# Attention logits of two head groups from half-height matmuls, value and retention products side by side

## The chip, the core and the metric

The kernel runs on one core of a Trainium2 chip. The metric is the device time of one execution in microseconds (us). TensorE multiplies (PE in the rows, with PEld for its weight loads), VectorE (DVE) and ScalarE (ACT) do the elementwise work, SyncE (SP) issues the DMAs. TensorE's results land in PSUM banks, which a program takes from a pool and gives back when the last reader is done.

## The reference, cut to what matters

Two layers over 256 tokens of width 1024. In each, one projection feeds eight attention heads (two groups g of four heads c; a group shares its keys and values) and eight retention heads:

```python
s_w = jnp.einsum('bqgrd,bgkd->bgrqk', qb, kwb)        # window branch; the selected branch likewise
p_w = masked_softmax(s_w - slopes[:, :, None, None] * dist_w, valid_w)
o_w = jnp.einsum('bgrqk,bgkd->bgrqd', p_w, vwb)
o = gb[0] * o_c + gb[1] * o_s + gb[2] * o_w           # gated sum of three branches
...
inner = jnp.einsum('bhnd,bhmd->bhnm', qi, ki) * decay_in   # retention
o = jnp.einsum('bhnm,bhme->bhne', inner, vi) + ...
```

With 256 tokens the selected branch picks every block and the window covers every key, so both are plain causal attention with a distance penalty. A dense SwiGLU follows in layer 0, eight experts (top 2) in layer 1, a gated per-layer embedding in both.

## The kernel before, in words

Everything runs in float32. Projections and other weight products are done as three fp32r products of a high and a low half (`mm3`, L207 to L209); the halves are made by ACT and DVE in `split` (L193, L194) from raw tiles that SP loads. Attention and retention use plain float32 products.

`mixer` does, in this order in the text: projections of values, keys and queries (`qT`, four tiles of 128 x 256, the two groups in partition halves); keys of the branches `br` 2 and 1 into `kz`, padded with zeros, so that group g's keys stand in its half of the partitions and the other half is zero; the compressed branch (L533 and after); then attention by query tile `t` (128 rows; t = 0 sees 128 keys, t = 1 sees 256), branch and group:

- logits, L572, four heads c as two pairs c2, each pair in one bank of `acc()`;
- row minima and the shifted logits, L576 on DVE, the exponential with its sum, L578 on ACT;
- scaling by gate over sum, L580 to L584 on DVE;
- transposes, L588, copied out of PSUM by ACT or DVE (L591, L593);
- the product with the values, L594, into half g of the columns of one bank;
- at the end of a tile the compressed branch's product, L604, and the copy into `mn` halves (L607, L608).

After attention come, in the text, three more projections that attention doesn't need: retention queries, keys and gates (240 products in all: 192 with 256 columns, 48 with 512). They take banks of `bank()`. Then retention: logits L648 and L657 over 64 partitions each, masked by decay on DVE (L650, L660), products with the values L668 and L670, and the output projection.

The order on each engine is set by a scheduler of the language, which moves instructions ahead of others in the text where their operands and buffers allow it. An engine executes its own queue in order. `bank()` and `acc()` are pools of four PSUM banks each, whose buffers are handed out in the order of the text: the fifth call gets the buffer of the first, once that is given back.

Of the kernel before, what the change touches and what calls it, by code (L numbers as in the profile page):

```python
# [92 lines left out]
def trunk(ctx: ExitStack, tc: tile.TileContext, a, cst, at, out, stop=None):  # L93
    nc = tc.nc
# [16 lines left out]
    def acc():  # L111
        w = psa.tile([128, 512], F32, name="acc")
        return w
# [267 lines left out]
    def mixer(i, pool, N, after, between, then, first, heads):  # L381
# [64 lines left out]
        kz = {}  # L446
        for br, src in ((2, pk[0]), (1, pk[1])):
            kz[br] = pool.tile([128, 2, S], F32, name=f"kz{br}")
            nc.gpsimd.memset(kz[br], 0.0)
            for g in range(2):  # L450
                gp = slice(g * 64, (g + 1) * 64)
                nc.vector.tensor_tensor(kz[br][gp, g], src[gp], R[gp], op=ALU.mult)
# [105 lines left out]
        for t in range(NT):  # L558
            nk = 128 * (t + 1)
            po = acc()  # L560
            pov = po.rearrange("p (c q) -> p c q", c=4)
            for bi, br in enumerate((2, 1)):
                for g in range(2):
                    P = brief.tile([128, 4, nk], F32, name="P", bufs=3)
                    mn = small.tile([128, 4], F32, name="mn")
                    sm = small.tile([128, 4], F32, name="sm")
                    for c2 in range(2):
                        pl = acc()
                        plv = pl[:, 0:2 * nk].rearrange("p (j k) -> p j k", j=2)
                        for j in range(2):  # L570
                            c = 2 * c2 + j
                            qk = nc.tensor.matmul(plv[:, j], qT[:, c, t * 128:(t + 1) * 128], kz[br][:, g, 0:nk],  # L572
                                             start=True, stop=True)
                        for j in range(2):
                            c = 2 * c2 + j
                            nc.vector.tensor_tensor_reduce(P[:, c], plv[:, j], K["dist"][:, 256 - nk:256], slope(g, c),  # L576
                                                           3e38, ALU.add, ALU.min, mn[:, c:c + 1])
                            nc.scalar.activation(P[:, c], P[:, c], AF.Exp, bias=mn[:, c:c + 1], scale=-1.0,  # L578
                                                 accum_out=sm[:, c:c + 1])
                    nc.vector.tensor_scalar(sm, sm, 1e-30, None, op0=ALU.max)  # L580
                    nc.vector.reciprocal(sm, sm)
                    nc.vector.tensor_tensor(sm, sm, gv[:, t, br, :, g], op=ALU.mult)
                    for c in range(4):
                        nc.vector.tensor_scalar(P[:, c], P[:, c], sm[:, c:c + 1], None, op0=ALU.mult)  # L584
                    for kc in range(t + 1):
                        pp = acc()
                        for c in range(4):
                            nc.tensor.transpose(pp[:, c * 128:(c + 1) * 128], P[:, c, kc * 128:(kc + 1) * 128], ident)  # L588
                        pT = brief.tile([128, 512], F32, name="pT", bufs=2)
                        if (g + kc) % 2:  # L590
                            nc.vector.tensor_copy(pT, pp)  # L591
                        else:
                            nc.scalar.copy(pT, pp)  # L593
                        nc.tensor.matmul(po[g * 64:(g + 1) * 64, :], vsw[:, kc, br - 1, g * 64:(g + 1) * 64], pT,  # L594
# [48 lines left out]
        A1 = pool.tile([128, 2, 4, 128], F32, name="xs")  # L643
        for s in range(2):
            p = acc()
            pw = p.rearrange("p (c n) -> p c n", c=4)
            for c in range(4):
# [709 lines left out]
```

## Time and profile before

| what | us |
|---|---|
| median of 3 runs | 1515.51 (1510.32 to 1520.99) |
| profiled execution, time | 1517.39 |
| its span, first to last instruction | 1515.6 |
| PE busy | 1449.3 (96%) |
| DVE busy, ACT busy | 642.1, 569.8 |
| mean granted TensorE clock | 0.987 |

Layer 0's mixer takes about 160 us of the span, layer 1's lies between 420 and 590 us, the experts fill the rest up to 1500 us, with the DMA engines near 100% busy there. A float32 matmul stands as two records in the trace, a transpose and an fp32r matmul as one. Records of PE overlap, so the distance from one start to the next tells what an instruction costs, not its length.

### The profile page before, as it was taken

To read this page: it belongs to the slowest core of one execution; us is meant where nothing else is said; L and a number is where in the kernel's file an instruction comes from. 1 tells how busy PE (TensorE), PEld (TensorE's weight loads), DVE (VectorE), ACT (ScalarE), POOL (GpSimd) and SP (SyncE) were. 2 spreads that over 40 slices of the span, in tenths; PEclk is the share of its full clock that TensorE was granted. 3 is DMA by queue.
4 is the path that set the end of the run, shared out by engine and by line. 5 is a ranking of instruction groups with operands and counts; after the bars stand their busy time and mean duration, and the time that the engine had idled before them with its cause. 6 is when DMAs were issued, how large, how long until landed. Compare 5 with 4: busy or idle time off the path is not lost. (4 is left out here: it accounts for less than half of the span.)

```text
span 1515.6 us, 30676 instructions
## 1 busy us (share of the span) xinstructions
PE 1449.3 (96%) x12570; PEld 832.9 (55%) x12570; DVE 642.1 (42%) x1459; ACT 569.8 (38%) x992; POOL 2.3 (0%) x8
## 2 busy tenths in 40 slices
PE   7999999999999999899999999999999999999987
PEld 6977899999889868433322232243333323323336
DVE  6765865555596767323222222222221322322337
ACT  5452544434464543333332332333233223223324
POOL 0000000000000000000000000000000000000000
PEclk9998999999999999899999999999999999999999
DMA  9923445555557513789999999999999999999971
GB/s 332 365 86 97 160 167 194 190 179 188 169 179 252 199 57 146 250 346 420 420 420 420 419 421 420 420 419 416 405 383 420 420 419 420 419 421 420 412 273 42
DMA packets 100621, 462.39 MB, mean 305 GB/s; under 512 B 9384, under 2 KB 20336, under 8 KB 57200
## 3 DMA queue, kind: packets, MB, share of 16 engines
q1 hardware_dynamic: 100224, 460.16, 77.5%
q8 instruction: 102, 1.67, 0.4%
q14 instruction: 55, 0.45, 0.1%
q10 hardware_dynamic: 240, 0.10, 0.0%
HBM read 459.19 MB, written 1.05 MB: 304 GB/s over the span
## 5 line engine op out<-in xcount | busy, mean ns | idle before, releaser
L1029 DVE COPY lo<-raw 128x512 f32 x333 | 140.7, 426 | 544.5 <-DMA raw<-in_moe_up 152.3
L1028 ACT COPY hi<-raw 128x512 f32 x333 | 204.0, 621 | 429.5 <-DMA raw<-in_moe_down 129.2
L194 DVE TENSOR_TENSOR lo<-raw,hi 128x1024 fp32r<-128x1024 f32 (+1 forms) x176 | 206.6, 1200 | 111.7 <-ACT hi L193 111.1
L193 ACT CAST hi<-raw 128x1024 fp32r<-128x1024 f32 (+1 forms) x176 | 175.0, 1031 | 170.0 <-issue 71.8
L1039 PE MATMUL w<-raw,xg 128*32 128x512 f32 x1744 | 211.5, 596 | 12.3 <-DMA raw<-in_moe_up 5.0
L1039 PE MATMUL acc<-raw,xg 128*32 128x512 f32 x1792 | 214.7, 596 | 2.5 <-DMA raw<-in_moe_gate 0.6
L207 PE MATMUL w<-xhi,hi 128*128 128x256 f32 x704 | 201.2, 286 | 0.3 <-ACT xhi L283 0.3
L209 PE MATMUL w<-xhi,lo 128*128 128x256 f32 x704 | 199.9, 284 | 0.0
L208 PE MATMUL w<-xlo,hi 128*128 128x256 f32 x704 | 199.7, 284 | 0.2 <-DVE xlo L284 0.2
L207 PEld LDWEIGHTS w<-xhi,hi 128*128 128x128 f32 x704 | 135.0, 192 | 2.4 <-issue 1.6
L208 PEld LDWEIGHTS w<-xlo,hi 128*128 128x128 f32 x704 | 135.0, 192 | 1.3 <-issue 0.8
L209 PEld LDWEIGHTS w<-xhi,lo 128*128 128x128 f32 x704 | 135.0, 192 | 0.8 <-issue 0.8
L1039 PE MATMUL acc<-raw,hT 128*32 128x512 f32 x960 | 116.6, 603 | 11.6 <-PEq L1225 6.6
L1039 PEld LDWEIGHTS w<-raw,xg 128*32 128x32 f32 x1744 | 51.8, 109 | 117.1 <-issue 66.2
L1039 PEld LDWEIGHTS acc<-raw,xg 128*32 128x32 f32 x1792 | 50.8, 109 | 98.7 <-issue 74.8
L1039 PE MATMUL w<-raw,hT 128*32 128x512 f32 x832 | 99.7, 597 | 4.8 <-DMA raw<-in_moe_down 1.4
L1039 PE MATMUL w<-hi,xg 128*32 128x256 f32 x448 | 72.8, 379 | 0.0
L1039 PE MATMUL w<-lo,xg 128*32 128x256 f32 x448 | 68.1, 379 | 0.0
L1039 PE MATMUL acc<-hi,xg 128*32 128x256 f32 x448 | 68.1, 379 | 0.0
L1039 PE MATMUL acc<-lo,xg 128*32 128x256 f32 x448 | 68.1, 379 | 0.0
L1039 PEld LDWEIGHTS acc<-raw,hT 128*32 128x32 f32 x960 | 28.4, 110 | 67.9 <-issue 38.0
L1039 PEld LDWEIGHTS acc<-hi,xg 128*32 128x32 f32 x448 | 27.6, 110 | 67.1 <-issue 55.9
(346 smaller groups left out, 1908.2 us busy)
## 6 DMA issues: line engine op xcount, KB each, us to landing
raw<-in_moe_gate SPq DMA_DIRECT2D x112, 1024.0 KB, 17.7
raw<-in_moe_down SPq DMA_DIRECT2D x112, 1024.0 KB, 17.8
raw<-in_moe_up SPq DMA_DIRECT2D x109, 1024.0 KB, 17.0
raw<-in_w_in SPq DMA_DIRECT2D x23, 1024.0 KB, 6.8
raw<-in_ffn_gate SPq DMA_DIRECT2D x14, 1024.0 KB, 5.1
raw<-in_ffn_up SPq DMA_DIRECT2D x14, 1024.0 KB, 5.1
raw<-in_ffn_down SPq DMA_DIRECT2D x14, 1024.0 KB, 5.0
raw<-in_cmp_w SPq DMA_DIRECT2D x8, 1024.0 KB, 8.8
```

What stands on the lines that cost most here:

```text
L193: order(nc.scalar.copy(hi[:, c], raw), b[0])
L194: order(nc.vector.tensor_tensor(lo[:, c], raw, hi[:, c].bitcast(F32), op=ALU.subtract), b[1])
L207: order(nc.tensor.matmul(o, l[0], r[0], start=start, stop=False, skip_group_check=skip), behind)
L208: nc.tensor.matmul(o, l[0], r[1], start=False, stop=False, skip_group_check=skip)
L209: nc.tensor.matmul(o, l[1], r[0], start=False, stop=stop, skip_group_check=skip)
L1028: nc.scalar.copy(hi, w[:, bass.ds(units[g][0], 1), :].rearrange("p e n -> p (e n)"))
L1029: nc.vector.tensor_copy(lo, w[:, bass.ds(units[g][1], 1), :].rearrange("p e n -> p (e n)"))
L1039: nc.tensor.matmul(P[b][o:o + UNIT, 0:WIDE[b]], x[:, b, o:o + UNIT], v, start=start, stop=stop, tile_position=(0, o), skip_group_check=True)
```

## The change

Keys are stored unpadded (`kT`, 128 x 256, both groups in their halves), so a group's logits are a product over 64 partitions instead of 128. The loop over groups moves inward: both groups' logits of a pair are issued alternately, group 0 into a bank of `acc()`, group 1 into one of `bank()`. The value products of the groups are issued next to each other, and so are retention's logits of the two partition halves. `P` and `pT` get four buffers, `mn` and `sm` too.

```diff
@@ -443,13 +443,10 @@
                     sp = R[g * 64:(g + 1) * 64, 0:1]
                     rv = bass.AP(tensor=sp.tensor, offset=sp.offset + par, ap=[sp.ap[0], [2, 16], [16, 15]])
                     nc.vector.tensor_tensor(dst, ap, rv, op=ALU.mult)
-        kz = {}
+        kT = {}
         for br, src in ((2, pk[0]), (1, pk[1])):
-            kz[br] = pool.tile([128, 2, S], F32, name=f"kz{br}")
-            nc.gpsimd.memset(kz[br], 0.0)
-            for g in range(2):
-                gp = slice(g * 64, (g + 1) * 64)
-                nc.vector.tensor_tensor(kz[br][gp, g], src[gp], R[gp], op=ALU.mult)
+            kT[br] = pool.tile([128, S], F32, name=f"kz{br}")
+            nc.vector.tensor_tensor(kT[br], src, R, op=ALU.mult)
 
 
         w = cols(1024, 512)
@@ -559,39 +556,45 @@
             nk = 128 * (t + 1)
             po = acc()
             pov = po.rearrange("p (c q) -> p c q", c=4)
+            rows = [slice(g * 64, (g + 1) * 64) for g in range(2)]
             for bi, br in enumerate((2, 1)):
-                for g in range(2):
-                    P = brief.tile([128, 4, nk], F32, name="P", bufs=3)
-                    mn = small.tile([128, 4], F32, name="mn")
-                    sm = small.tile([128, 4], F32, name="sm")
-                    for c2 in range(2):
-                        pl = acc()
-                        plv = pl[:, 0:2 * nk].rearrange("p (j k) -> p j k", j=2)
+
+                P = [brief.tile([128, 4, nk], F32, name="P", bufs=4) for g in range(2)]
+                mn = [small.tile([128, 4], F32, name="mn", bufs=4) for g in range(2)]
+                sm = [small.tile([128, 4], F32, name="sm", bufs=4) for g in range(2)]
+                for c2 in range(2):
+                    plv = [p[:, 0:2 * nk].rearrange("p (j k) -> p j k", j=2) for p in (acc(), bank())]
+                    for j in range(2):
+                        c = 2 * c2 + j
+                        for g in range(2):
+                            qk = nc.tensor.matmul(plv[g][:, j], qT[rows[g], c, t * 128:(t + 1) * 128],
+                                                  kT[br][rows[g], 0:nk], start=True, stop=True)
+                    for g in range(2):
                         for j in range(2):
                             c = 2 * c2 + j
-                            qk = nc.tensor.matmul(plv[:, j], qT[:, c, t * 128:(t + 1) * 128], kz[br][:, g, 0:nk],
-                                             start=True, stop=True)
-                        for j in range(2):
-                            c = 2 * c2 + j
-                            nc.vector.tensor_tensor_reduce(P[:, c], plv[:, j], K["dist"][:, 256 - nk:256], slope(g, c),
-                                                           3e38, ALU.add, ALU.min, mn[:, c:c + 1])
-                            nc.scalar.activation(P[:, c], P[:, c], AF.Exp, bias=mn[:, c:c + 1], scale=-1.0,
-                                                 accum_out=sm[:, c:c + 1])
-                    nc.vector.tensor_scalar(sm, sm, 1e-30, None, op0=ALU.max)
-                    nc.vector.reciprocal(sm, sm)
-                    nc.vector.tensor_tensor(sm, sm, gv[:, t, br, :, g], op=ALU.mult)
+                            nc.vector.tensor_tensor_reduce(P[g][:, c], plv[g][:, j], K["dist"][:, 256 - nk:256],
+                                                           slope(g, c), 3e38, ALU.add, ALU.min, mn[g][:, c:c + 1])
+                            nc.scalar.activation(P[g][:, c], P[g][:, c], AF.Exp, bias=mn[g][:, c:c + 1], scale=-1.0,
+                                                 accum_out=sm[g][:, c:c + 1])
+                for g in range(2):
+                    nc.vector.tensor_scalar(sm[g], sm[g], 1e-30, None, op0=ALU.max)
+                    nc.vector.reciprocal(sm[g], sm[g])
+                    nc.vector.tensor_tensor(sm[g], sm[g], gv[:, t, br, :, g], op=ALU.mult)
                     for c in range(4):
-                        nc.vector.tensor_scalar(P[:, c], P[:, c], sm[:, c:c + 1], None, op0=ALU.mult)
-                    for kc in range(t + 1):
+                        nc.vector.tensor_scalar(P[g][:, c], P[g][:, c], sm[g][:, c:c + 1], None, op0=ALU.mult)
+                for kc in range(t + 1):
+                    pT = []
+                    for g in range(2):
                         pp = acc()
                         for c in range(4):
-                            nc.tensor.transpose(pp[:, c * 128:(c + 1) * 128], P[:, c, kc * 128:(kc + 1) * 128], ident)
-                        pT = brief.tile([128, 512], F32, name="pT", bufs=2)
+                            nc.tensor.transpose(pp[:, c * 128:(c + 1) * 128], P[g][:, c, kc * 128:(kc + 1) * 128], ident)
+                        pT.append(brief.tile([128, 512], F32, name="pT", bufs=4))
                         if (g + kc) % 2:
-                            nc.vector.tensor_copy(pT, pp)
+                            nc.vector.tensor_copy(pT[g], pp)
                         else:
-                            nc.scalar.copy(pT, pp)
-                        nc.tensor.matmul(po[g * 64:(g + 1) * 64, :], vsw[:, kc, br - 1, g * 64:(g + 1) * 64], pT,
+                            nc.scalar.copy(pT[g], pp)
+                    for g in range(2):
+                        nc.tensor.matmul(po[rows[g], :], vsw[:, kc, br - 1, rows[g]], pT[g],
                                          start=(bi == 0 and kc == 0), stop=False, tile_position=(0, 64 * g),
                                          skip_group_check=True)
             if t == 0:
@@ -641,23 +644,22 @@
         nc.sync.dma_start(dec, cst["decay"])
         dv = dec.rearrange("p (s c n) -> p s c n", s=2, c=4)
         A1 = pool.tile([128, 2, 4, 128], F32, name="xs")
+        half = [slice(s * 64, (s + 1) * 64) for s in range(2)]
+        pw = [acc().rearrange("p (c n) -> p c n", c=4) for s in range(2)]
+        for c in range(4):
+            for s in range(2):
+                nc.tensor.matmul(pw[s][:, c], krT[half[s], c, 128:256], qrT[half[s], c, 128:256], start=True, stop=True)
         for s in range(2):
-            p = acc()
-            pw = p.rearrange("p (c n) -> p c n", c=4)
-            for c in range(4):
-                nc.tensor.matmul(pw[:, c], krT[s * 64:(s + 1) * 64, c, 128:256], qrT[s * 64:(s + 1) * 64, c, 128:256],
-                                 start=True, stop=True)
-            nc.vector.scalar_tensor_tensor(A1[:, s], pw, rs[1], dv[:, s, :, 0:128], op0=ALU.mult, op1=ALU.mult)
+            nc.vector.scalar_tensor_tensor(A1[:, s], pw[s], rs[1], dv[:, s, :, 0:128], op0=ALU.mult, op1=ALU.mult)
         for c2 in range(2):
+            pw = [acc().rearrange("p (c n) -> p c n", c=2) for s in range(2)]
+            for j in range(2):
+                c = 2 * c2 + j
+                for s in range(2):
+                    nc.tensor.matmul(pw[s][:, j], krT[half[s], c, 0:128], qrT[half[s], c, :], start=True, stop=True)
             for s in range(2):
-                p = acc()
-                pw = p.rearrange("p (c n) -> p c n", c=2)
-                for j in range(2):
-                    c = 2 * c2 + j
-                    nc.tensor.matmul(pw[:, j], krT[s * 64:(s + 1) * 64, c, 0:128], qrT[s * 64:(s + 1) * 64, c, :],
-                                     start=True, stop=True)
                 dc = dv[:, s, 2 * c2:2 * c2 + 2]
-                nc.vector.scalar_tensor_tensor(dc, pw, rs[0], dc, op0=ALU.mult, op1=ALU.mult)
+                nc.vector.scalar_tensor_tensor(dc, pw[s], rs[0], dc, op0=ALU.mult, op1=ALU.mult)
         cens = pool.tile([128, NT, 8, 64], F32, name="qrT")
         cen, var = [], pool.tile([128, NT, 8], F32, name="var")
         for t in range(NT):
```

The scheduler places much else anew. First place: PE's queue in layer 0 from the compressed branch's logits to the first value product of t = 0. `w_` are banks of `bank()`, `acc_` of `acc()`; L207 to L209 on `w_1022` and `w_1023` are the first of the 240 later projection products. Before:

```order
L533 MATMUL acc_670<-var_659,qT_517 128x32 x8
L572 MATMUL acc_700<-kz2_395,qT_517 128x128 x2
...
L572 MATMUL acc_707<-kz2_395,qT_517 128x128 x2
L207 MATMUL w_1022<-xhi_104,hi_1008 128x256
L208 MATMUL w_1022<-xlo_105,hi_1008 128x256
L209 MATMUL w_1022<-xhi_104,lo_1009 128x256
...
L588 MATMUL acc_721<-pack_80,P_697 128x128
...
L594 MATMUL acc_696<-pT_726,vsw_646 64x512
L572 MATMUL acc_732<-kz2_395,qT_517 128x128 x2
L572 MATMUL acc_739<-kz2_395,qT_517 128x128 x2
L207 MATMUL w_1022<-xhi_104,hi_1016 128x256
```

Now, where L570 stands for L572, L590 for L588 and L597 for L594:

```order
L530 MATMUL acc_666<-var_655,qT_513 128x32 x8
L570 MATMUL acc_699<-kz2_395,qT_513 128x128 x2
L570 MATMUL w_764<-kz1_397,qT_513 128x128
L570 MATMUL acc_713<-kz2_395,qT_513 128x128 x2
L570 MATMUL w_764<-kz1_397,qT_513 128x128
L570 MATMUL w_778<-kz1_397,qT_513 128x128 x2
L570 MATMUL w_840<-kz2_395,qT_513 128x256 x2
L570 MATMUL w_854<-kz2_395,qT_513 128x256 x2
L590 MATMUL acc_741<-pack_80,P_693 128x128 x4
L590 MATMUL acc_748<-pack_80,P_694 128x128 x3
L597 MATMUL acc_692<-pT_746,vsw_642 64x512
L590 MATMUL acc_748<-pack_80,P_694 128x128
```

What moved: between L533 (now L530) and the last compressed product of t = 0 (L604, now L607) the queue held 144 of the 240 projection products in layer 0, in layer 1 171; now it holds none in either. Of the logits of t = 1, eight of sixteen products (all of group 1) now stand inside t = 0. Logits of the two groups stand in runs of one group, and change from one group to the other without other work between only at three places, all in t = 0.

Second place: PE's queue in layer 0 from the last value products of t = 1 to retention. Before:

```order
L594 MATMUL acc_836<-pT_986,vsw_646 64x512
L594 MATMUL acc_836<-pT_994,vsw_646 64x512
L604 MATMUL acc_836<-us0_828,th_668 128x128 x4
...
L209 MATMUL w_1257<-hi_1250,xlo_105 128x512
L648 MATMUL acc_1316<-qrT_1120,gb_1237 128x128 x4
L648 MATMUL acc_1322<-qrT_1120,gb_1237 128x128 x4
L657 MATMUL acc_1328<-qrT_1120,gb_1237 128x256 x2
L657 MATMUL acc_1332<-qrT_1120,gb_1237 128x256 x2
L657 MATMUL acc_1336<-qrT_1120,gb_1237 128x256 x2
L657 MATMUL acc_1340<-qrT_1120,gb_1237 128x256 x2
```

Now, where L651 stands for L648 and L670 for L668:

```order
L597 MATMUL acc_832<-pT_982,vsw_642 64x512
L597 MATMUL acc_832<-pT_989,vsw_642 64x512
L607 MATMUL acc_832<-us0_824,th_664 128x128 x4
L208 MATMUL w_1018<-xlo_105,hi_1012 128x256
L209 MATMUL w_1018<-xhi_104,lo_1013 128x256
...
L209 MATMUL w_1253<-hi_1246,xlo_105 128x512
L651 MATMUL acc_1312<-qrT_1116,gb_1233 128x128
L651 MATMUL acc_1313<-qrT_1116,gb_1233 128x128
L651 MATMUL acc_1312<-qrT_1116,gb_1233 128x128
...
L670 MATMUL acc_1342<-vr_139,xn_1309 128x64
```

What moved: 155 projection products now stand between attention's last product and retention's first, where 4 stood; 85 stand inside t = 1. The value products stand next to each other at two places for each layer (one in each branch of t = 1); elsewhere transposes or logits lie between them. Retention's first 12 logit products alternate between the halves. Layer 1 has the same order now; before, its last projection product stood ahead of attention's last value products.

Third place: DVE's queue around retention in layer 0, now (before, the order was L608, L637, L650, L194, L637, L650, L660, and no `split` stood between L608 and L637):

```order
L611 TENSOR_TENSOR kz2_998<-acc_832,kz1_997 128x512
L194 TENSOR_TENSOR lo_1239<-raw_1236,hi_1238 128x1024 x2
...
L194 TENSOR_TENSOR lo_1433<-raw_1430,hi_1432 128x1024 x2
L640 SCALAR_TENSOR_TENSOR qT_1302<-th_1303,w_1252 128x512
L194 TENSOR_TENSOR lo_1519<-raw_1516,hi_1518 128x1024
L640 SCALAR_TENSOR_TENSOR qT_1302<-th_1306,w_1253 128x512
L653 SCALAR_TENSOR_TENSOR xs_1311<-acc_1312,r1_223,xn_1309 128x512
L653 SCALAR_TENSOR_TENSOR xs_1311<-acc_1313,r1_223,xn_1309 128x512
L662 SCALAR_TENSOR_TENSOR xn_1309<-acc_1324,r0_205,xn_1309 128x512
```

What moved: eight halves of `split` (L194) for the late projections follow attention now, and both gate products (L640) with one more half stand ahead of both masked logits (L653).

## Rows read from the trace of the kernel before

**Rows 1.** Windows by stage: us, busy time by engine (instructions), clock, DMA share, GB/s
```profile
64.30:95.40 31.10, 30.95 (x227) 26.63 (x225) 23.09 (x89) 17.80 (x50) 0.00 (x0) 1.00 0.58 214
...
95.40:131.30 35.90, 35.88 (x178) 24.84 (x176) 20.86 (x67) 16.56 (x45) 0.00 (x0) 1.00 0.27 88
...
131.30:147.70 16.40, 15.14 (x86) 14.24 (x85) 8.76 (x12) 2.88 (x4) 0.00 (x0) 0.67 0.30 97
...
563.60:579.00 15.40, 15.40 (x105) 13.57 (x104) 11.40 (x21) 2.95 (x6) 0.00 (x0) 1.00 0.30 103
```

**Rows 2.** Timeline of PE, layer 0: start, length, line, tiles, count
```profile
64.33 1.95 PE L533 MATMUL acc<-var,qT 128*128 128x32 f32 x16
...
69.00 0.28 PE L209 MATMUL w<-xhi,lo 128*128 128x256 f32 x1
...
69.12 0.28 PE L207 MATMUL w<-xhi,hi 128*128 128x256 f32 x1
...
76.07 1.16 PE L572 MATMUL acc<-kz,qT 128*128 128x128 f32 x8
...
76.98 0.37 PE L207 MATMUL w<-xhi,hi 128*128 128x256 f32 x1
...
91.74 1.03 PE L572 MATMUL acc<-kz,qT 128*128 128x256 f32 x4
...
92.69 1.07 PE L594 MATMUL acc<-pT,vsw 128*64 128x512 f32 x2
...
93.70 1.16 PE L604 MATMUL acc<-us,th 128*128 128x128 f32 x8
...
111.51 1.93 PE L594 MATMUL acc<-pT,vsw 128*64 128x512 f32 x4
```

**Rows 3.** Timeline of DVE, layer 0, attention of t = 0
```profile
67.03 0.28 DVE L576 CUSTOM_DVE_ANT_0 P<-acc,pack 128x128 f32<-128x128 f32 x1
...
72.17 0.47 DVE L584 TENSOR_SCALAR P<-P,sm 128x128 f32<-128x128 f32 x2
...
78.83 0.17 DVE L580 TENSOR_SCALAR sm<-sm 128x4 f32<-128x4 f32 x1 [1.06 <-ACT P L578]
...
79.45 0.87 DVE L584 TENSOR_SCALAR P<-P,sm 128x128 f32<-128x128 f32 x4
```

**Rows 4.** Timeline of ACT, layer 0: the copy of a transposed tile
```profile
74.42 0.59 ACT L593 COPY pT<-acc 128x512 f32<-128x512 f32 x1 [0.66 <-PE acc L588]
```

**Rows 5.** Windows of half a us and one us after layer 0's attention
```profile
134.50:135.00 0.50, 0.00 (x0) 0.00 (x0) 0.50 (x2) 0.00 (x0) 0.00 (x0) 1.00 0.00 0
...
137.00:137.50 0.50, 0.50 (x4) 0.50 (x4) 0.50 (x1) 0.00 (x0) 0.00 (x0) 0.51 0.00 0
...
150.00:151.00 1.00, 1.00 (x5) 0.82 (x4) 0.75 (x2) 0.28 (x1) 0.00 (x0) 0.67 0.00 0
```

**Rows 6.** Timeline of PE, layer 0, around retention
```profile
130.76 0.40 PE L208 MATMUL w<-lo,xhi 128*128 128x512 f32 x1
...
130.99 0.40 PE L209 MATMUL w<-hi,xlo 128*128 128x512 f32 x1
...
131.32 1.37 PE L648 MATMUL acc<-qrT,gb 64*128 64x128 f32 x13
...
136.77 0.49 PE L668 MATMUL acc<-vr,xn 128*128 128x64 f32 x2
...
147.69 0.77 PE L207 MATMUL acc<-hi,mnh 128*128 128x512 f32 x1
```

**Rows 7.** Timeline of PE, layer 1: attention's start, retention's value products, what follows
```profile
494.45 1.87 PE L533 MATMUL acc<-var,qT 128*128 128x32 f32 x16
...
567.25 0.43 PE L668 MATMUL acc<-vr,xn 128*128 128x64 f32 x2
...
573.70 0.47 PE L207 MATMUL acc<-hi,mnh 128*128 128x512 f32 x1
```

**Rows 8.** Timeline of DVE, layer 0, after attention's last product
```profile
131.78 0.68 DVE L637 SCALAR_TENSOR_TENSOR qT<-th,w 128x512 f32<-128x512 f32 x1
...
135.57 2.72 DVE L660 SCALAR_TENSOR_TENSOR xn<-acc,r,xn 128x512 f32<-128x512 f32 x4
```

## The prediction, written before the changed kernel ran

> **What bounds the kernel now.** I read the windows by stage first. In the attention of layer 0 PE is busy 30.95 of 31.10 us and 35.88 of 35.90 us, with DVE at 23.09 and 20.86 and the DMA share at 0.58 and 0.27 [rows 1]. PE is the bound there, and its queue is in order, so the stage is the sum of what stands in that queue plus every wait that nothing covers. The reader is to see that there is no such wait today: the softmax of one group takes several us on DVE and ACT, and PE fills them with projection products that attention doesn't need. What the change does to that cover matters as much as what it does to the products. After attention the picture differs: in 131.30 to 147.70 PE is idle for 1.3 us and its granted clock averages 0.67 [rows 1]. The stages before and after the mixers keep their instructions, so a later start of what follows shifts them whole.
>
> **Prices on PE** come from distances between starts. A projection product of 256 columns costs 0.12 (69.00 to 69.12). Four logit products over 128 keys cost 0.91 (76.07 to 76.98), 0.23 each; two over 256 keys 0.95 (91.74 to 92.69), 0.475 each; one value product 1.01 alone (92.69 to 93.70), and two in a row 1.93 [rows 2].
>
> **What the change removes on PE.** On paper much: per layer 16 logits of 0.23 and 16 of 0.475 are 11.3 us, twelve value products some 11.5, retention's logits some 5.1 (8 of 0.23, 8 of 0.4). Were each pair to run at once, half of it, 13.9, would go. But a pair can only overlap if the two stand next to each other in PE's in-order queue. By the new order value products do so in two of six pairs: 2 x 0.93 = 1.9 us saved for each layer, if columns 0 to 63 and 64 to 127 work at once; 0 if not. Logits change group without other work between only three times: 0 to 0.7, I take 0. Retention's first twelve alternate, worth some 2.5 us of PE, but DVE's queue decides there (below), so 0 on the path. Two of four key multiplications and the memsets go, in a stretch where PE is full: 0.
>
> A half-height product puts PE in another arrangement of the array. Before retention this costs 0.1: a 512-column projection starts 0.23 before the next (130.76, 130.99), and the first L648 comes 0.33 after the last one [rows 6]. The Trainium skill, page "TensorEngine Tiling (Array Packing)", section "Key Properties", says that changing the tiling mode drains the engine. By it each such change costs; by the row 0.1 for some 16 new changes, 1.6 us for each layer, most of it in waits. I take 0 and keep 1.6 for the upper end.
>
> **What it moves.** The late projections take banks of the pool that group 1's logits now take before them in the text. So they follow in the queue: none of 144 (layer 0) remains in t = 0. I rebuild t = 0 of layer 0 without them.
>
> Block one (branch 2). DVE starts the minima at 67.03, as now, and was done scaling one group at 72.17 + 0.47 = 72.6. The second group adds four minima of 0.28, three small operations (78.83 to 79.45) and four scalings, 0.87: 2.6 us, so 75.2 [rows 3]. Group 0 is scaled 1.5 us earlier; its transposes and copy (0.59, [rows 4]) take 0.9, its value product runs from 74.7 to 75.7, then group 1's last transpose and the logits of branch 1 start at 75.8.
>
> Block two. Now one group needs from the start of its logits (76.07, [rows 2]) to the end of its scaling (79.45 + 0.87 = 80.32, [rows 3]) 4.25 us; the second adds 0.62 + 0.87 = 1.5. So group 0 is scaled at 80.05, group 1 at 81.55. Then in queue order: 0.9 to group 0's copy, its value product until 81.95, transposes 0.55, a logit pair 0.95, group 1's value product 1.0, the compressed product 1.0: 85.5. I say 86.
>
> Before, t = 0 ended at 93.70 + 1.0 = 94.7 [rows 2]. It ends 8.7 us sooner, but 144 x 0.12 = 17.3 us of projection is still to do, less what moved into the gaps: eight logits of t = 1, 8 x 0.475 = 3.8. From there to retention took 131.32 - 94.7 = 36.6 us with PE full [rows 2, 6]. Now: 36.6 + 17.3 - 3.8 - 1.9 = 48.2, plus waits in t = 1, where PE has some 23 us of work, 85 projections among it, against two softmax chains of some 12 us: 0 to 4, I take 1.3. Retention starts at 86 + 49.5 = 135.5 instead of 131.3.
>
> **Retention itself.** Today the first masked product L668 starts 5.45 us after the first L648 [rows 6], and DVE's row tells why: from 131.78 to 135.57 it works through gate, mask, split, gate, mask before L660 [rows 8]. These wait for ACT's tanh of the last projection. The new order has the same operations behind the last projection, so I keep 5.5: L670 at 141.0, against 136.77: **+4.2** in layer 0.
>
> Layer 1 gets the same order, so the same stage: from L533 to the first masked product 141.0 - 64.33 = 76.7 [rows 2] instead of 567.25 - 494.45 = 72.8 [rows 7], **+3.9**. And it loses something else. In layer 0 PE stood idle before 135.7, and the clock fell to 0.51 in the window at 137.0 and came back in the one at 150.0 [rows 5]; masked products until the output projection took 147.69 - 136.77 = 10.9 us [rows 6]. In layer 1 PE had no idle time there, the clock stayed 1.00 [rows 1], and they took 6.45 [rows 7]. Now layer 1's last projection also ends right before retention, with the same wait for tanh and DVE. I expect layer 1 to look like layer 0: 10.9 - 6.45 = 4.5, and some 0.5 for the output products at half clock: **+5**.
>
> **The clock inside t = 0.** Layer 0's row shows the clock halved after half-height logits with one idle stretch of over a us [rows 5, 6]. The new t = 0 has half-height logits and several waits, the longest some 2 us before the first transposes. I think the clock falls there too. On its path then lie a value product, logits and transposes of block one, 1.75 us at full clock, and 7.8 us at the end of block two (two logit pairs ahead of the transposes, 1.9, transposes 1.0, two value products 2.0, two logit pairs 1.9, the compressed product 1.0). At half clock these cost as much again: 1.75 if the clock is back for block two, 9.5 if it returns with the projections only. I take 5.5 for each layer, since PE is dense again from the first value product on: **+11**. DVE and ACT don't slow with it.
>
> **Sum.** 4.2 + 3.9 + 5 + 11 = 24 on the profiled execution's 1517.39 (span 1515.6 plus 1.8 around it): 1541.5. That execution is 1.9 above the median of the runs, so against 1515.5 it is 1539.5, say **1540**.
>
> **The rivals.**
>
> *The clock holds in t = 0.* For it: PE has some 17 us of work in these 22. Against it: the row at 137.0. It gives 13 more than before, 1529; without the fall in layer 1's retention too, 1524.
>
> *The clock stays down until the projections.* For it: in layer 0's retention it stayed down from 137.0 to 150, with PE busy all the time [rows 1, 5]. Then 9.5 instead of 5.5 for each layer, and with the drains 1550.
>
> *The pairs do what they say* and the time falls. The Trainium skill, page "TensorE: Matmul & The Clock Gate", section "Part 3: Packing small matmuls — row/col tiling", says that matmuls in different row groups run at once, their starts some 4 ns apart. As a mechanism of this kernel: 13.9 us less PE work for each layer, 27.8 in all, 1488, if waits stay covered. Against it: the order sets most partners apart, and retention's pairs meet DVE's queue. It decides the sign once it saves more for each layer than the 8.6 us that t = 0 falls behind (17.3 less 8.7).
>
> *The chain in t = 0 is shorter than I rebuilt it*, down to PE's own 17 us: then each layer loses 5 less at full clock, and with a steady clock in t = 0 the whole is 1515 to 1520, no change.
>
> **How the numbers follow.** Forecast 0.50 (1532 to 1546); clock holds 0.22; clock stays down 0.16; shorter chain 0.08; pairs 0.04. A measurement of this kernel tells about 1%, 15 us, from no change. Faster by more: 0.03 (the pairs). Same: the shorter chain, most of the holding clock, a little of the forecast, 0.28. Slower: 0.69. The range leaves out the pairs, most of the shorter chain and the far tails: 1521 to 1556.
>
> **What would show it.** No L207 to L209 on PE between the first logits and the compressed product of t = 0, with t = 0 about 22 us long (more at half clock) and PE idle for some 5 of them; granted clock 0.5 inside it and, in layer 1, after the late projections; retention in layer 0 starting at 135 or later; the expert phase shifted whole. I am wrong if t = 0 stays near 17 us, if the clock stays at 1.00, or if logits of both groups overlap in spite of their order.

## The result, and the profile of the changed kernel

The changed kernel takes **1538.2 us** (median, 1537.77 to 1539.32) against 1513.2 of the kernel before on the same chip: ratio **1.0153**, interval 1.0115 to 1.019 (estimated over all runs, so it isn't the quotient of the medians). Forecast were 1540, range 1521 to 1556, slower. The profiled execution is 1537.77 (span 1536.0, mean clock 0.976), 20.4 above that of before; in both profiles the clock halves behind retention in layer 0 and holds in layer 1. To read the runs, one thing has to be known: in some executions the clock halves behind retention in one layer or in both, which costs 6 to 7 us for each, 5 of them in the masked products, so that runs of before lie near 1510 or near 1517.

Lines of after: L530 is L533 of before, L570 L572, L575 L576, L590 L588, L597 L594, L607 L604, L651 and L659 L648 and L657, L653 and L662 L650 and L660, L670 L668. Windows by stage come first: layer 0 from L530 to the last compressed product of t = 0, t = 1, the late projections, retention to the first masked product, masked products; then the same five of layer 1, without the two that repeat.

```profile
64.67:93.55 28.88, 27.56 (x95) 16.88 (x94) 17.44 (x88) 10.83 (x42) 0.00 (x0) 0.59 0.40 152
93.55:118.52 24.97, 24.97 (x156) 18.04 (x155) 16.20 (x59) 12.25 (x37) 0.00 (x0) 1.00 0.13 43
118.52:142.35 23.83, 23.83 (x157) 21.66 (x155) 10.31 (x9) 11.29 (x14) 0.00 (x0) 1.00 0.44 136
142.35:147.79 5.44, 4.17 (x35) 3.15 (x34) 4.94 (x7) 2.68 (x4) 0.00 (x0) 1.00 0.46 178
147.79:158.20 10.41, 10.41 (x52) 10.41 (x52) 3.35 (x5) 0.00 (x0) 0.00 (x0) 0.53 0.47 153
507.20:533.40 26.20, 21.79 (x97) 12.94 (x96) 17.63 (x88) 10.98 (x42) 0.00 (x0) 0.80 0.35 132
...
582.23:587.67 5.44, 4.17 (x35) 3.14 (x35) 4.94 (x7) 2.67 (x4) 0.00 (x0) 1.00 0.40 169
587.67:593.40 5.73, 5.73 (x52) 5.73 (x52) 3.34 (x5) 0.00 (x0) 0.00 (x0) 1.00 0.59 193
```

Compare the counts. PE ran 227 instructions in the 31.1 us around t = 0 of before [rows 1], and 95 in the 28.9 of now: t = 0 is hardly shorter, though all its projection products are gone. They are in the third row, 23.8 us of nothing else, where before retention's first logits (131.32, [rows 6]) came 2.0 us after the start of attention's last product:

```profile
127.44 1.93 PE L594 MATMUL acc<-pT,vsw 128*64 128x512 f32 x4
129.30 1.16 PE L604 MATMUL acc<-us,th 128*128 128x128 f32 x8
```

PE's share still reads 27.56 of 28.88: with the clock at 0.59 the same products just take longer, and a busy PE hides the loss. The timeline of PE in layer 0 (start, length, line, tiles, count; a float32 product counts twice):

```profile
64.67 2.01 PE L530 MATMUL acc<-var,qT 128*128 128x32 f32 x16
...
69.85 3.78 PE L570 MATMUL w<-kz,qT 64*128 64x256 f32 x8 [0.57 <-DVE mn L575]
73.92 1.86 PE L590 MATMUL acc<-pack,P 128*128 128x128 f32 x7 [0.28 <-DVE P L584]
75.70 1.97 PE L597 MATMUL acc<-pT,vsw 128*64 128x512 f32 x2
77.60 0.47 PE L590 MATMUL acc<-pack,P 128*128 128x128 f32 x1
...
87.40 1.97 PE L597 MATMUL acc<-pT,vsw 128*64 128x512 f32 x2 [0.46 <-ACT pT L595]
...
116.51 1.08 PE L597 MATMUL acc<-pT,vsw 128*64 128x512 f32 x4
117.52 1.16 PE L607 MATMUL acc<-us,th 128*128 128x128 f32 x8
...
146.08 1.79 PE L659 MATMUL acc<-qrT,gb 64*128 64x256 f32 x8 [1.27 <-DVE xs L653]
147.79 0.43 PE L670 MATMUL acc<-vr,xn 128*128 128x64 f32 x2
```

One value product takes 1.90 in t = 0 (75.70 to 77.60), nearly twice its full-clock price of 1.01, and two side by side take 1.01 at 116.51 (to 117.52), where before two took 1.86 (127.44 to 129.30). The named waits in t = 0 are short. One-us windows of the same stretch say when the clock went (the last four numbers of a row are POOL, clock, DMA share, GB/s):

```profile
65.00:66.00 1.00, 1.00 (x11) 1.00 (x10) 1.00 (x2) 0.99 (x4) 0.00 (x0) 1.00 1.04 414
66.00:67.00 1.00, 1.00 (x10) 0.94 (x10) 0.85 (x4) 0.45 (x1) 0.00 (x0) 0.73 1.03 410
67.00:68.00 1.00, 1.00 (x9) 1.00 (x9) 0.65 (x4) 0.00 (x0) 0.00 (x0) 0.50 1.01 401
...
90.00:91.00 1.00, 1.00 (x5) 0.71 (x5) 0.69 (x1) 0.35 (x1) 0.00 (x0) 0.82 0.00 0
```

It fell within 66 to 67 (by tenths of a us between 66.4 and 66.5), before the first wait, with PE busy throughout, and came back within 90 to 91. What PE ran just before were products of 16 and 64 columns, four half-height logits from 63.54 on and the 32-column products of L530. In layer 1 it fell twice, within 513 to 514 after a wait of 1.49 and within 527 to 528, and was back at 521 and 531.

Where the 20.4 are, from the starts of the same instructions in both kernels: layer 0 from L530 to the first masked product 83.1 instead of 72.4, **+10.7**; masked products 10.4 instead of 10.9, -0.5; from there to layer 1's L530 349.0 instead of 346.8, **+2.2**; layer 1's mixer to the first masked product 80.5 instead of 72.8, **+7.7**; its masked products 5.7 instead of 6.5, -0.7; the rest +0.7; the later start of L530 itself +0.3.

### The profile page after: what moved, and what is told of

Its sections match the earlier page's. It is cut to its first block, busy times and chain, and to the rows that moved or that the text cites. A ratio compares the mean times of both kernels' runs of the same rounds, so it can differ in the third digit from the quotient of the medians.

```text
span 1536.0 us, 30651 instructions
## 1 busy us (share of the span) xinstructions
PE 1464.9 (95%) x12570; PEld 838.2 (55%) x12570; DVE 639.6 (42%) x1455; ACT 570.2 (37%) x992; POOL 0.2 (0%) x4
## 5 line engine op out<-in xcount | busy, mean ns | idle before, releaser
L194 DVE TENSOR_TENSOR lo<-raw,hi 128x1024 fp32r<-128x1024 f32 (+1 forms) x176 | 206.6, 1200 | 130.9 <-ACT hi L193 130.4
L207 PE MATMUL w<-xhi,hi 128*128 128x256 f32 x704 | 200.0, 285 | 0.3 <-ACT xhi L283 0.3
L209 PE MATMUL w<-xhi,lo 128*128 128x256 f32 x704 | 199.9, 284 | 0.0
L207 PEld LDWEIGHTS w<-xhi,hi 128*128 128x128 f32 x704 | 134.9, 192 | 1.4 <-issue 0.7
L209 PEld LDWEIGHTS w<-xhi,lo 128*128 128x128 f32 x704 | 135.0, 192 | 0.7 <-issue 0.7
L1041 PE MATMUL w<-hi,xg 128*32 128x256 f32 x448 | 72.8, 379 | 0.0
```

What stands on the lines that cost most here:

```text
L194: order(nc.vector.tensor_tensor(lo[:, c], raw, hi[:, c].bitcast(F32), op=ALU.subtract), b[1])
L207: order(nc.tensor.matmul(o, l[0], r[0], start=start, stop=False, skip_group_check=skip), behind)
L209: nc.tensor.matmul(o, l[1], r[0], start=False, stop=stop, skip_group_check=skip)
L1041: nc.tensor.matmul(P[b][o:o + UNIT, 0:WIDE[b]], x[:, b, o:o + UNIT], v, start=start, stop=stop, tile_position=(0, o), skip_group_check=True)
```

## The experiments

Three kernels stand on a line from before to after: both groups and retention's halves side by side with all else as before, then without the projections in t = 0, then with half-height keys.

**Only the banks put back.** In the changed kernel one word:

```diff
-                    plv = [p[:, 0:2 * nk].rearrange("p (j k) -> p j k", j=2) for p in (acc(), bank())]
+                    plv = [p[:, 0:2 * nk].rearrange("p (j k) -> p j k", j=2) for p in (acc(), acc())]
```

> The changed kernel, but group 1's logits take a bank of acc() like group 0's, not of bank(). By the program's order 110 projection products stand in t = 0 of layer 0 again and 56 are left for after attention. Theory 'cover' (the time went because the late projections' banks come after the logits' in the pool, so nothing covers the softmax chains of t = 0): PE full again through attention, clock 1.00 there, and the pairs that do stand side by side save some 5 us in each layer; about 1507 us, between 1500 and 1516, against 1513 of before. Rival 'half height' (products over 64 partitions and their changes of arrangement cost, and pull the clock down): stays at 1530 or more.

Measured: 1508.65, ratio 0.9971 (0.9947 to 0.9995). PE's queue of t = 0 in layer 0 holds 110 projection products again, and every one-us window of attention shows the clock at 1.00. All that the changed kernel loses hangs on that word: without it the change costs nothing and may gain a little. (Its profile, at 1520.4, shows the clock halved behind retention in both layers.)

**Padded keys, banks put back.** The former kernel with `kz` of before, its memsets and four multiplications, and logits over all 128 partitions.

```diff
-                            qk = nc.tensor.matmul(plv[g][:, j], qT[rows[g], c, t * 128:(t + 1) * 128],
-                                                  kT[br][rows[g], 0:nk], start=True, stop=True)
+                            qk = nc.tensor.matmul(plv[g][:, j], qT[:, c, t * 128:(t + 1) * 128],
+                                                  kz[br][:, g, 0:nk], start=True, stop=True)
```

> e1_acc with padded keys: both groups side by side from acc(), logits over 128 partitions as before. If half-height pairs pay more than their changes of arrangement cost (some 3.5 us saved against some 1.8 for each layer): attention of layer 0 some 1.7 us longer than e1_acc's 64.8 from the compressed logits to retention, about 1512 us against 1508.7. If the changes cost more: shorter, about 1505.

Measured: 1508.96, ratio 0.9947 (0.9933 to 0.9961); beside the former kernel the height of the keys is worth nothing here. Two rows of each, the former kernel first, then the padded one, tell why: four records are two products, a pair.

```profile
87.05 0.70 PE L570 MATMUL acc<-kz,qT 64*128 64x256 f32 x4
87.68 1.07 PE L597 MATMUL acc<-pT,vsw 128*64 128x512 f32 x2
```

```profile
86.85 1.13 PE L573 MATMUL acc<-kz,qT 128*128 128x256 f32 x4
87.91 1.07 PE L600 MATMUL acc<-pT,vsw 128*64 128x512 f32 x2
```

A pair whose partners meet takes 0.63 instead of 1.06. But t = 0 is 25.84 with half height and 25.91 with full, t = 1 27.02 and 27.20: where they meet they gain, and what they gain is as good as lost elsewhere. The side-by-side order itself is a gain: L533 to retention takes 65.1 in the padded kernel, against 67.0 before [rows 2, 6], about what two pairs of value products save, 2 x 0.85 = 1.7. More than half of the 8.0 us between the two profiles lies elsewhere, behind retention in layer 0, where the padded kernel's clock held: from the first masked product to layer 1's L533 352.8 instead of 357.7.

**Padded keys, banks as changed.** The same edit in the changed kernel, its `bank()` left as it is; PE's queue in attention has instruction for instruction the order of the changed kernel.

> The changed kernel with padded keys again, so every logit product has its full height of 128; the banks of the pool, and so PE's whole order in attention, stay those of the changed kernel, without a projection product in t = 0. It asks whose fault the fall of the clock in t = 0 is. Half-height theory: the clock falls because half-height logits stand in a row without projections between them; with full height it stays at 1.00 through t = 0, whose length goes from 28.9 to 22 to 24 us, and the kernel comes to 1524 to 1530. Filler theory: it falls for want of the dense projections, whatever the height of the logits; it falls again between 66 and 74, t = 0 stays at 27 to 29.5 us, and the kernel at 1534 to 1542.

Measured: 1527.95, ratio 1.0092 (1.0068 to 1.0117). Windows of t = 0, retention and masked products in layer 0, and of t = 0 in layer 1:

```profile
63.40:85.62 22.22, 18.29 (x95) 12.07 (x96) 17.23 (x88) 10.83 (x42) 0.00 (x0) 1.00 0.53 204
...
134.38:140.18 5.80, 4.53 (x35) 3.19 (x35) 5.30 (x8) 2.67 (x4) 0.00 (x0) 0.93 0.43 164
140.18:151.08 10.90, 10.90 (x52) 10.90 (x52) 2.99 (x4) 0.00 (x0) 0.00 (x0) 0.50 0.44 146
498.91:523.75 24.84, 20.76 (x99) 13.46 (x98) 17.92 (x89) 11.22 (x42) 0.00 (x0) 0.86 0.38 145
```

In layer 0 the clock stays at 1.00 through t = 0, though PE waits 1.35 us at a time in it, and t = 0 takes 22.2 us: the 22 that the prediction rebuilt for a full clock. With half-height keys the same order takes 28.9. The runs agree with the profiles: the five of this kernel take 1527.7 to 1529.5 (mean clock 0.985), the four of the changed one 1537.8 to 1539.3 (0.975 to 0.976). So the half-height theory holds for layer 0, as to what has to be there for the fall. How it comes about stays open: only four half-height logits stood ahead of the 32-column products in which the clock fell, and in layer 1 of the changed kernel it held through the same place. In layer 1 the theory doesn't hold: there the clock fell with full height too, within 508 to 509, behind a wait of 2.36 us:

```profile
508.73 1.86 PE L593 MATMUL acc<-pack,P 128*128 128x128 f32 x7 [2.36 <-DVE P L587]
```

From 1509.0 to 1528.0 is what the missing projections cost, 19 at most: of the 19.4 between the profiles, 6.3 are in layer 0's mixer up to the first masked product and 8.2 in layer 1's, while 5.9 lie behind retention in layer 0, where this kernel's clock halved and the former's held; that the missing projections cause that fall too is not shown. From 1528.0 to 1538.2, 10, is what half height adds once they are missing: of the 8.9 between the profiles, 6.4 are in layer 0's mixer and 1.1 in layer 1's.

**The projections held back, nothing else.** The kernel before, with the late projections of queries and keys ordered behind the compressed product of t = 0:

```diff
+                pm = nc.tensor.matmul(pov[:, c], vb[:, 2 * c:2 * c + 2].rearrange("p g d -> p (g d)"), pcT[:, t],
...
+            if t == 0:
+                held = pm
...
-                     for c in range(4)])
+                     for c in range(4)], held)
```

> The kernel before with one thing alone: the late query and key projections are held in PE's queue behind the last compressed product of t = 0. No half-height logits in attention, no pairs. 'Cover': four softmax chains of some 4.5 us stand bare, t = 0 ends near 89 us instead of 94.7 with 144 products still to do, 12 us behind for each layer, and 2 to 10 more for each if the clock falls: 1537 to 1558 us. 'Half height': no reason for a loss, 1513.

Measured: 1542.12, ratio 1.0182 (1.0157 to 1.0206). Full-height keys, no pairs, and as slow as the changed kernel. Its windows of t = 0 in both layers, and two waits on PE:

```profile
62.87:92.10 29.23, 19.73 (x87) 12.49 (x88) 17.33 (x84) 11.07 (x42) 0.00 (x0) 0.77 0.39 154
501.18:532.20 31.02, 21.55 (x86) 14.14 (x87) 18.61 (x85) 12.09 (x43) 0.00 (x0) 0.61 0.32 123
```

```profile
70.22 1.50 PE L588 MATMUL acc<-pack,P 128*128 128x128 f32 x4 [4.44 <-DVE P L584]
...
78.70 0.30 PE L588 MATMUL acc<-pack,P 128*128 128x128 f32 x1 [2.33 <-DVE P L584]
```

Group by group the softmax of every block is waited for, 4.44, 2.33, 1.01 and 0.93 in layer 0; side by side, with the same loss of projections, the longest such wait there is 1.35, and the kernel comes to 1528.0 (full height in both).

**Half-height keys alone.** The kernel before, group by group, with `kT` made as in the change:

```diff
-                            qk = nc.tensor.matmul(plv[:, j], qT[:, c, t * 128:(t + 1) * 128], kz[br][:, g, 0:nk],
-                                             start=True, stop=True)
+                            qk = nc.tensor.matmul(plv[:, j], qT[g * 64:(g + 1) * 64, c, t * 128:(t + 1) * 128],
+                                             kT[br][g * 64:(g + 1) * 64, 0:nk], start=True, stop=True)
```

> The kernel before with one part of the change alone: unpadded keys, logits over 64 partitions, group by group as before. The program's order is that of before. 'Cover': no change, 1513 us, at most 4 more for the changes of arrangement. 'Half height': slower by 10 to 25, 1523 to 1538, with the clock below 1.00 in attention.

Measured: 1523.81, ratio 1.0049 (1.003 to 1.0068). The clock is 1.00 through attention, yet L533 to retention takes 71.2 in layer 0 instead of 67.0, and L533 to the end of the last compressed product 71.5 instead of 68.4 in layer 1. Rows of t = 0:

```profile
75.74 1.16 PE L569 MATMUL acc<-kz,qT 64*128 64x128 f32 x8
76.82 0.39 PE L207 MATMUL w<-xhi,hi 128*128 128x256 f32 x1
77.05 0.28 PE L208 MATMUL w<-xlo,hi 128*128 128x256 f32 x1
...
79.55 0.30 PE L585 MATMUL acc<-pack,P 128*128 128x128 f32 x1
79.78 0.49 PE L569 MATMUL acc<-kz,qT 64*128 64x128 f32 x2
80.19 0.55 PE L585 MATMUL acc<-pack,P 128*128 128x128 f32 x3
```

Four products take 1.08 before the next projection starts, instead of 0.91 [rows 2]; one between transposes 0.41 instead of 0.23. Over all blocks of one to four products the addition is 0.1 to 0.4 and doesn't grow with their number, so it goes with the block and not with the product: each change into half height and out of it costs something. All blocks of logits together take 13.6 instead of 9.7 in layer 0 (16 blocks) and 13.4 instead of 10.2 in layer 1 (15), 3 to 4 us for each layer, nearly the whole loss in attention. That is the rule of the Trainium skill, page "TensorEngine Tiling (Array Packing)", section "Key Properties", that the prediction weighed; these rows agree with it, and give it a price above my upper end of 1.6.

**Retention's pairs alone**, in the kernel before: the last part of the change's diff, and nothing else of it.

> The kernel before with the retention part of the change alone: logits of both partition halves issued alternately. By the step 'DVE's queue decides there' nothing changes: 1513 us within 3, the first masked product (L667) still some 5.4 us after retention's first logits in layer 0. By the rival that the pairs are worth what PE saves: 2.5 us less in each layer, 1508.

Measured: 1516.49, ratio 1.0007 (0.9995 to 1.002). PE's rows in layer 0:

```profile
131.48 1.16 PE L648 MATMUL acc<-qrT,gb 64*128 64x128 f32 x16
132.47 1.03 PE L656 MATMUL acc<-qrT,gb 64*128 64x256 f32 x8
...
135.39 1.78 PE L656 MATMUL acc<-qrT,gb 64*128 64x256 f32 x8 [1.34 <-DVE xs L650]
137.11 0.43 PE L667 MATMUL acc<-vr,xn 128*128 128x64 f32 x2
```

Eight products in 0.99: the pairs do overlap. Then PE waits for DVE, and the first masked product comes 5.63 after the first logits, against 5.45 [rows 6].

**Dense products put into t = 0.** The changed kernel with 24 products of 256 columns, which compute nothing that is used, behind the first block's logits:

```diff
+                if t == 0 and bi == 0:
+                    for k in range(24):
+                        d = order(nc.tensor.matmul(po[:, 0:256], x[0][:, k % 8, 0:128], x[0][:, k % 8, :], start=True, stop=True,
+                                                   skip_group_check=True), qk)
```

> The changed kernel plus 24 dense products of 256 columns in t = 0 of each layer, behind the first block's logits in PE's queue, into a bank that the first value product overwrites. They compute nothing and fill part of the bare wait. If the halved clock is a part of the loss: clock back (layer 0) or kept (layer 1) in t = 0, that stage 28.9 to some 26 and 26.2 to some 23.5 us, in all 1530 to 1534 us, still well above 1513. If the bare waits are all of it: 1538 or later.

Measured: 1544.02, ratio 1.0186 (1.0172 to 1.02). The rows of layer 0: the 24 products, and the windows where the clock came back and fell again.

```profile
68.18 4.82 PE L581 MATMUL acc<-xhi 128*128 128x256 f32 x24
```

```profile
71.00:72.00 1.00, 1.00 (x7) 1.00 (x7) 1.00 (x3) 0.59 (x4) 0.00 (x0) 0.50 0.81 324
72.00:73.00 1.00, 1.00 (x9) 0.86 (x8) 1.00 (x9) 0.00 (x0) 0.00 (x0) 0.98 0.12 49
...
82.00:83.00 1.00, 0.52 (x3) 0.06 (x1) 0.63 (x4) 1.00 (x6) 0.00 (x0) 0.64 0.00 0
```

With them the clock was back at 72, for ten us. It had fallen within 65 to 66 (0.61), again while L530 ran and before any wait. But the 24 products ran at half clock themselves, 4.8 us that stand ahead of attention's own products, and t = 0 takes 27.9 instead of 28.9, in layer 1 27.7 instead of 26.2. The median lies where the bare waits alone were expected (1538 or later), but this try doesn't separate the clock's share from its own cost; the padded kernel above does. Why the median is another 6 us higher than the changed kernel's stays open; half-clock retention, which fell on layer 1 in its profile, is one part that varies.

**Value products behind both groups.** The kernel before, group by group, padded, its projections where they were; only the value products of a branch are issued after both groups' transposes, with six buffers for `pT`:

```diff
-                        pT = brief.tile([128, 512], F32, name="pT", bufs=2)
+                        pT = brief.tile([128, 512], F32, name="pT", bufs=6)
...
-                        nc.tensor.matmul(po[g * 64:(g + 1) * 64, :], vsw[:, kc, br - 1, g * 64:(g + 1) * 64], pT,
+                        pTs[g, kc] = pT
+                for kc in range(t + 1):
+                    for g in range(2):
+                        nc.tensor.matmul(po[g * 64:(g + 1) * 64, :], vsw[:, kc, br - 1, g * 64:(g + 1) * 64], pTs[g, kc],
```

> The kernel before with the value products alone moved: group by group as before with padded keys, but a branch's value products issued after both groups, so that partners can stand together (they do in two to four places for each layer). 25 projections are left behind attention. By the step 'a pair saves 0.93 us' 1.9 to 3.7 us less for each layer, less up to 4 in layer 1 where tanh is bare: 1508 to 1513 us.

Measured: **1503.46**, ratio 0.9912 (0.9899 to 0.9926), better than both kernels. PE's last value products of t = 1, three in 1.86, and the windows of retention and the masked products in layer 0:

```profile
118.88 1.93 PE L598 MATMUL acc<-pT,vsw 128*64 128x512 f32 x6
120.74 1.16 PE L608 MATMUL acc<-us,th 128*128 128x128 f32 x8
```

```profile
127.53:131.84 4.31, 4.18 (x33) 3.31 (x32) 3.80 (x6) 2.67 (x4) 0.00 (x0) 1.00 0.61 225
131.84:141.40 9.56, 9.56 (x70) 8.92 (x70) 7.26 (x12) 1.33 (x2) 0.00 (x0) 1.00 0.51 166
```

L533 to retention takes 64.5 instead of 67.0 in layer 0, and to the first masked product 68.8 instead of 72.4. In retention PE is busy 4.18 of 4.31 us, where it idled 1.3 us before [rows 1], and the clock behind it stays at 1.00 in both layers. That clock is about half of the gain: of the 13.4 us between the profiles 6.5 lie between layer 0's first masked product and layer 1's L533, 351.2 instead of 357.7, and 350.9 is what this stretch takes in the retention-pairs kernel, whose clock held in the order of before. What is left, some 7 us, is the order's. That the clock holds because PE no longer waits in retention would fit all five runs (1502.7 to 1504.7), but it is not shown.

**Six buffers alone**, the first line of that diff.

> The kernel before with six buffers for the transposed weights pT instead of two, and nothing else: a control for the run that issues the value products in pairs and came to 1503.5. If the gain there is the pairs' (two value products in 1.0 us instead of 1.93), this one shows no change, 1510 to 1518. If the buffers alone free PE's queue, it comes to 1503 to 1507 too.

Measured: 1517.61, ratio 1.0019 (1.0003 to 1.0034). The buffers alone gain nothing, so the gain comes with the order of the value products.

## Why the prediction was right, step by step

- *No projections in t = 0, which then takes 22 us at full clock.* Right: 22.2 in layer 0 of the padded kernel with the changed banks. That this is the cause of the loss is shown from both sides, by the banks put back (1508.7) and by before with its projections held (1542.1).
- *The debt, +4.2 in layer 0.* From L533 to the first masked product the padded kernel with the changed banks takes 76.8, against 72.4: 4.3 before rounding, of which 0.4 is retention at a clock of 0.93. Retention's chain of 5.5 measured 5.44 in both layers of the changed kernel.
- *The clock inside t = 0, +5.5 for each layer.* In layer 0 6.7 (28.9 less 22.2). The size was nearly right, the reason wrong in two points. I put the fall at the waits; it came before any of them, and with full height the same order kept its clock through longer waits. So the half-height products are what the fall needed there; why, no run tells. And I let the clock come back with the first value product; it stayed at half until 90 to 91, as the rival *the clock stays down until the projections* has it. PE's work in t = 0 took 27.56 instead of 18.29, 9.3 more and close to that rival's 9.5, but 2.6 of it filled waits: PE idles 1.3 us in t = 0 of the changed kernel and 3.9 in that of the padded one. In layer 1 it isn't measured against an undisturbed row: with layer 0's 22.2 it would be 4.0, less whatever its longer waits cost at any clock; full height saw a fall there too.
- *Layer 1's retention clock, +5.* This step failed: that stretch measured 0.7 less than before. I took the fall for a consequence of the idle time in retention. In the changed kernel PE idles 1.27 us there in both layers, and the clock fell in layer 0 and not in layer 1; in the padded kernel with its banks put back, it fell in neither. The same wait goes either way, and what decides it stays open.
- *Why the sum still fits.* On the profiled execution 24.1 were forecast before rounding and 20.4 came. Too much were 5.7 in layer 1's retention and 1.7 in the rest of its mixer (7.7 instead of 3.9 + 5.5). Too little were 1.0 in layer 0's mixer (10.7 instead of 4.2 + 5.5) and 2.7 in places for which I had no step: 2.2 between the mixers, 0.7 after layer 1's, 0.3 ahead of layer 0's, less 0.5 in layer 0's masked products. The cause of the 2.2 stays open; the other side-by-side kernels show 0.3 to 1.4 there. So terms that were off by more than the remaining error cancelled, which is luck. More of it lies in the median: I took off 1.9 because the profiled execution of before lay above its median, while that of the changed kernel lies 0.4 below its own; 3.7 too much on the profile became 1.8.
- *A change of mode costs 0, at most 1.6.* Mis-sized in general: 3 to 4 us for each layer where half-height logits stand alone among other work. With the groups side by side and the banks put back, half height and full height come to the same time, so there the pairs that meet earn it back; for the order of the changed kernel no run prices it by itself.
- *Value pairs save 0.93 at two places for each layer; retention's pairs nothing.* Right in place and sign. For 0.93 I used a record's length, 1.93; by starts two in a row took 1.86, so a pair saves 0.85. Retention's pairs gained nothing (1.0007).
- *Logits of the two groups don't overlap.* I counted such an overlap among the signs of being wrong, and it is there. In t = 0 of layer 1 products of the two groups start 0.01 apart:

```profile
509.10 0.37 PE L570 MATMUL acc<-kz,qT 64*128 64x128 f32 x1
509.11 0.37 PE L570 MATMUL w<-kz,qT 64*128 64x128 f32 x1
```

The nine products from there on are done in 1.4 us, against 2.3 in the padded kernel with the same banks. It changed nothing in the sum: PE waits 1.49 for DVE right behind them.

Of the rivals, *the clock holds* (1529, 1524) is what the padded kernel with the changed banks does in layer 0. That it came to 1528.0 is in part chance, since in its layer 1 the clock fell in t = 0 and held behind retention. *The chain is shorter* fails: 22.2 is as long as I rebuilt it. *The pairs do what they say* fails as expected on the order: two pairs of value products save 1.7 us for each layer.

## What to carry to other kernels

Where an engine's queue is full because one stage's waits are filled with another stage's work, ask of every change which pool its buffers come from: here one `acc()` written as `bank()` put the projections of t = 0 behind attention and cost 19 us with full-height keys and 30 with half-height ones (some 6 of each are retention's clock in layer 0), while nothing in the arithmetic changed. Pairs are worth only what stands next to its partner in the queue, so issue partners back to back and leave the filler where it is: the value products alone, paired so, gained 0.9%, about half of it because the clock behind retention held. And when PE reads as full, look at the granted clock beside it before calling the stage bound by its work.

## What the hardware did that was not expected

- The clock fell from 1.00 to 0.50 within one us while PE was busy in every window around it (66 to 68 in layer 0 of the changed kernel), after half-height and 32-column products; the same instructions did it in the kernel with dense products added (65 to 66); the same order with full-height logits kept 1.00 through waits of 0.85, 0.44 and 1.35 us.
- For the same instructions in the same order the clock behind retention fell or held from layer to layer and from one kernel to the next: masked products took 10.9 and 10.6 in the two layers of the kernel with its banks put back, 10.4 and 5.7 in the changed kernel, 5.7 and 10.9 in that with dense products added, 5.7 and 5.7 in the padded one with its banks put back, after 1.27 us of idle PE each time.
